# Softmax weights times values for two heads in one step, on the two halves of the array's columns

## The chip, the cores and the metric

One core of a Trainium2 chip runs the whole program. The metric is device time in microseconds (us), the median over executions. Five engines matter here: PE (TensorE, matmuls; its weight loads are shown apart as PEld), DVE (VectorE), ACT (ScalarE), POOL (GpSimd) and SP, which issues the weight loads.

## The reference, cut to what matters

Two transformer blocks over 256 tokens of width 1024. Three of their attentions have heads whose values are 64 wide, and these three are what the change touches:

```python
# first block, sliding window: 8 query heads over 2 key/value heads, d = 64
s = jnp.einsum('bnqhgd,bnkhd->bnhgqk', qb, kw).astype(jnp.float32) * scale
...
p = e / (jnp.sum(e, axis=-1, keepdims=True) + jnp.exp(sink - m))
o = jnp.einsum('bnhgqk,bnkhd->bnqhgd', p.astype(v.dtype), vw)

# second block, layer 0 (hybrid): 8 heads, values 64 wide
p = masked_softmax(s, kpos[None, :] <= qpos[:, None])
return jnp.einsum('bhqk,bkhd->bqhd', p.astype(v.dtype), v)

# second block, layer 1: 16 heads over 2 key/value heads, three branches added with gates
o_c = jnp.einsum('bgrqn,bngd->bqgrd', p_c.astype(dt), v_cmp)
o_s = jnp.einsum('bgrqk,bgqkd->bqgrd', p_s.astype(dt), vs)
o_w = jnp.einsum('bgrqk,bkgd->bqgrd', p_w.astype(dt), vw)
```

With 256 tokens the selected branch (`o_s`) and the window branch (`o_w`) of layer 1 are plain causal attentions; `o_c` is a small one over 15 compressed keys. Everything else is projections, feed-forwards, norms and residuals.

## The kernel before, in words

The weights (some 300 MB) are streamed from memory in units of 1 MB. Each unit is split into a high part (ACT, tile `whi`) and a low part (DVE, tile `wlo`, line 404), and a product with weights is three matmuls, high by high, low by high, high by low (tile `mm`). 24 such matmuls belong to one weight step. Attention works in plain float32, and a float32 matmul leaves two weight loads and two matmul records in the trace, one for each of its passes.

The program is a list of steps in one order, and each engine carries out its part of them in that order; nothing is rescheduled. For one head with 64 value columns there are four steps:

- S: `scores` (line 791) puts the mask and q·k into a PSUM tile `sc` (two buffers), and `softmax` (line 801) takes the maxima on DVE (`nm`, lines 806 and 807) and the exponentials on ACT (`p`);
- N: `scale_p` (line 834) inverts the sums on DVE (`r`, lines 829 and 831) and multiplies the weights by them (line 838);
- T: `transp` (line 841) turns the weights over with three matmuls against the identity (PSUM tile `pT`, two buffers) and copies them to `pTs` (three buffers), on DVE (line 330) or ACT in turn;
- P: `pv` (line 850) multiplies them with the values (tile `v` or `va`) into one half of the partitions of a PSUM tile `o`: 64 value columns are the stationary operand, so the product takes 64 of the array's 128 columns, the lower half for one head of a pair and the upper one for the other. All 256 queries take part with the first 128 keys, and the last 128 queries with the other keys. After the second head, `split_out` (line 885) takes `o` into two parts `oh` (ACT) and `ol` (DVE) for the output product.

`rounds` (line 271) makes the order: in round r it puts T of item r-3, P of item r-5, S of item r and N of item r-1 (lags 0, 1, 3, 5; for layer 1 of the second block the table `NLAGS` = 0, 1, 4, 6 is used, line 45). The three places are:

- the sliding window heads of the first block (`sP`, line 1142; list made at line 1154), 8 items, spread by `merge` among weight steps (line 1265);
- the hybrid layer (`mP`, line 1538; line 1548), 8 items, spread among four weight steps, then the last `HY` = 14 steps among two (line 1553);
- layer 1 (`nP`, line 1718; line 1740), 32 items in the order pair j, branch b, half g; six weight steps are put into rounds 0, 1, 4, 5, 10 and 13 (`NFILL`), and two more among the last `NS` = 20 steps (line 1749). After both branches of a pair of heads, one matmul with `cpT` and `vcz` adds the compressed branch to the same `o`.

Of the kernel before, what the change touches and what calls it, by code (L numbers as in the profile page):

```python
# [24 lines left out]
P = 128  # L25
# [25 lines left out]
# ------------------------------------------------------------------ host layout  # L51
def _tiles(w):
    """[K, M] -> [K/128, M/128, 128, 128]"""
    K, M = w.shape
    return w.reshape(K // P, P, M // P, P).transpose(0, 2, 1, 3)


def _units(seq):
    """sequence of [128, n] blocks (given as [T, 128, n]) -> [128, T * n], 16 tiles a unit"""
# [7 lines left out]
def pack_pairs(w):  # L67
    """column tiles in pairs, k outside the pair"""
    t = _tiles(w)
    K, M = t.shape[:2]  # L70
    t = t.reshape(K, M // 2, 2, P, P).transpose(1, 0, 2, 3, 4)
    return _units(t.reshape(-1, P, P))


def pack_cols(w):
    """column tiles one after the other, k inside"""
# [4 lines left out]
def early_order(K, M):  # L81
    """(column tile, row tile) in turn: the first half of the rows for the first half of the columns comes first"""
# [12 lines left out]
def pack_rows(w, kk):  # L95
    """kk row tiles a unit, all columns of each"""
# [5 lines left out]
def pack_ada(w):  # L102
    """for each modulation row, units of two row tiles"""
# [4 lines left out]
def cols(v):  # L108
    """[n * 128] -> [128, n]"""
# [131 lines left out]
# ------------------------------------------------------------------ kernel  # L241
# [6 lines left out]
class Two:  # L248
    """two [P, S] tiles seen as one [P, 2, S]"""
# [8 lines left out]
def merge(a, b):  # L258
    """two lists of steps, each in its order, spread evenly over one another"""
# [11 lines left out]
def rounds(n, *stages, lags=(0, 1, 3, 5)):  # L271
    """the stages of n items, each stage so many rounds behind the first; later stages first in a round"""
    out = []
    for r in range(n + lags[-1]):
        for k in (2, 3, 0, 1):
            i = r - lags[k]
            if 0 <= i < n:
                out += stages[k](i)
    return out


class Kernel:
# [12 lines left out]
    # ---- small helpers  # L295
# [6 lines left out]
    def t(self, name, shape=None, dt=F):  # L302
        """short-lived"""
# [16 lines left out]
    def table(self, func):  # L320
        """loads the table of a function ahead of its use"""
# [4 lines left out]
    def copy(self, out, in_):  # L326
        """PSUM -> SBUF on whichever of the two engines had less"""
# [19 lines left out]
    def mm3(self, out, w, x, start, stop, swap=False):  # L347
        """float32 product of operands in two parts; w stationary unless swap"""
# [7 lines left out]
    # ---- the stream of weights  # L356
    def stream_init(self, steps):
        """loads in the order of use, but raw units behind the next LEAD split ones"""
# [54 lines left out]
    def second(self):  # L413
        """the low part of the last split, one split behind its high part"""
# [35 lines left out]
    # ---- products with weights  # L450
    def pairs(self, name, x, kc, evac, unit0=0, npairs=None, st=None, head=0, tags=("mm", "mm"),
              biased=None):
        """steps: column tiles in pairs, k outside; evac(pair, psum [P, 2, S]); the first head pairs are of
        activations not yet normed (their norm's state in st), with the shift in two columns behind them"""
# [50 lines left out]
    def singles(self, name, x, kc, evac, early=False):  # L505
        """steps: column tiles one by one, k inside; evac(m, psum [P, S]); early: half of the columns start on
        the first half of the activations"""
# [25 lines left out]
    def rowsteps(self, name, x, width, evac, unit0=0, nk=8, kk=4, sub_k=2, tags=("mm", "mm")):  # L533
        """steps: the activations stationary, [tokens, width] out; evac(token block, psum)"""
# [18 lines left out]
    # ---- norms over the features (which lie on partitions)  # L553
    # The products that follow a norm start on x * gain; what the norm divides by is per token, so it is
    # applied to their results, or to the activations once it is there.
    def norm_part(self, st, c, n, xc, gain, dst=None):
        """one chunk's share of the sum of squares, and the chunk times its gain in two parts"""
# [67 lines left out]
    def along(self, out, by):  # L625
        """the factors of the tokens, which lie on partitions, along the free axis of every partition"""
# [3 lines left out]
    def norm_bc(self, st, scale=1.0):  # L630
        """what the norm multiplies by, along the tokens; and the results that waited for it"""
# [7 lines left out]
    def norm_apply(self, st, gain, shift, c0, c1):  # L639
        """the activations themselves, over those not normed"""  # L640
# [1186 lines left out]
```

## Time and profile before

| | |
|---|---|
| runs, median (lowest to highest) | 1501.49 us (1499.78 to 1502.46), 3 runs |
| profiled execution, span from first to last instruction | 1497.7 us |
| PE busy, weight loads busy | 97%, 92% |
| DVE, ACT, POOL busy | 71%, 61%, 42% |
| the sliding window heads' stretch of the trace, first P to behind the last | 75.30 to 114.70 us |
| the hybrid heads' stretch, first S to behind the last P | 699.70 to 735.60 us |
| layer 1's stretch, first P to behind the last | 1202.70 to 1278.20 us |

The profiled execution has no other time of its own than its span, which lies 3.8 us under the median of the runs. "Busy" of PE counts matmul records whose ends are modelled, so the time from one start to the next says more than the busy time.

### The profile page before, as it was taken

What the parts mean: (1) busy time and instruction counts of PE and PEld (TensorE: products, weight loads), DVE (VectorE), ACT (ScalarE), POOL (GpSimd) and SP (SyncE); (2) the same over time, 40 slices, a digit from 0 to 9 for tenths busy, and PEclk for the clock granted to TensorE, in tenths of its full rate; (3) what the DMA queues carried; (4) which work ended last, traced back from release to release, by engine and by line L of the source; (5) the groups of instructions that cost most, each with busy time, mean ns of one, the idle gap of its engine ahead of it and who ended that gap; (6) DMA issues with size and microseconds to landing.
All of it is one profiled execution on the core that took longest, in us unless ns stands there. A gap on an engine that the chain in (4) does not pass through costs nothing.

```text
span 1497.7 us, 28352 instructions
## 1 busy us (share of the span) xinstructions
PE 1454.4 (97%) x11478; PEld 1384.8 (92%) x11478; DVE 1056.4 (71%) x1643; ACT 918.8 (61%) x1666; POOL 635.8 (42%) x466
## 2 busy tenths in 40 slices
PE   8998999999999999998999999999999999999997
PEld 8887989999989989997899999899999877999997
DVE  7967767776658777679887676677665777764553
ACT  6546766777657567664677666576654555654442
POOL 3102433545874567753546659466553200500021
PEclk9999999999999999999999999999999999999999
DMA  8344646677665777654548777577754510355551
GB/s 316 117 141 165 211 159 226 245 268 277 250 253 194 292 255 272 253 195 165 182 172 289 275 277 259 204 274 279 288 215 175 197 57 5 137 197 183 184 174 51
DMA packets 46067, 312.00 MB, mean 208 GB/s; under 512 B 5232, under 2 KB 7024, under 8 KB 9072
## 3 DMA queue, kind: packets, MB, share of 16 engines
q1 hardware_dynamic: 45936, 310.19, 57.7%
q8 instruction: 90, 1.47, 0.4%
q14 instruction: 41, 0.34, 0.1%
HBM read 309.12 MB, written 1.05 MB: 207 GB/s over the span
## 4 chain that ended last, share of the span: by engine, by line
PE 69%; DVE 15%; ACT 7%; DMA 5%; issue 3%; POOL 2%; SPq 0%; POOLq 0%; ACTq 0%; DVEq 0%
PE mm L345 59%; DVE wlo L404 5%; DMA raw<-w 3%; PE o L345 3%; PE sc L345 2%; ACT whi L318 2%; POOL adacc L726 2%; ACT raw L318 1%; PE mmt L345 1%; DVE hlo L653 1%; PE pT L845 1%; DVE hlo L563 1%; PE ada L345 1%; DVE gl L342 1%; DMA raw<-w_up 1%
## 5 line engine op out<-in xcount | busy, mean ns | idle before, releaser
L404 DVE TENSOR_TENSOR wlo<-raw,whi 128x1024 fp32r<-128x1024 f32 (+2 forms) x438 | 625.5, 1434 | 51.0 <-ACT whi L318 50.4
L726 POOL TENSOR_TENSOR adacc<-adacc,raw 128x512 f32<-128x512 f32 x252 | 431.9, 1739 | 415.5 <-ACT raw L318 338.8
L345 PE MATMUL mm<-hlo,whi 128*128 128x256 f32 x1960 | 556.8, 284 | 4.5 <-DVE hlo L653 4.1
L345 PE MATMUL mm<-hhi,whi 128*128 128x256 f32 (+1 forms) x1960 | 558.4, 285 | 1.1 <-ACT whi L318 1.1
L345 PE MATMUL mm<-hhi,wlo 128*128 128x256 f32 (+1 forms) x1960 | 553.4, 282 | 4.6 <-DVE wlo L404 4.6
L318 ACT ACTIVATE whi<-raw 128x1024 fp32r<-128x1024 f32 (+2 forms) x438 | 453.1, 1044 | 112.6 <-DMA raw<-w 75.3
L345 PEld LDWEIGHTS mm<-hlo,whi 128*128 128x128 f32 x1960 | 370.1, 189 | 8.3 <-DVE hlo L653 5.6
L345 PEld LDWEIGHTS mm<-hhi,wlo 128*128 128x128 f32 x1960 | 371.2, 189 | 7.0 <-DVE wlo L404 6.6
L345 PEld LDWEIGHTS mm<-hhi,whi 128*128 128x128 f32 x1960 | 370.3, 189 | 5.1 <-issue 2.5
L345 PE MATMUL mm<-gh,whi 128*128 128x256 f32 x960 | 272.6, 284 | 0.0
L345 PE MATMUL mm<-gh,wlo 128*128 128x256 f32 x960 | 271.6, 283 | 0.0
L345 PE MATMUL mm<-gl,whi 128*128 128x256 f32 x960 | 271.6, 283 | 0.0
L345 PEld LDWEIGHTS mm<-gh,whi 128*128 128x128 f32 x960 | 184.2, 192 | 4.3 <-issue 3.4
L345 PEld LDWEIGHTS mm<-gl,whi 128*128 128x128 f32 x960 | 184.2, 192 | 0.0
L345 PEld LDWEIGHTS mm<-gh,wlo 128*128 128x128 f32 x960 | 184.2, 192 | 0.0
L318 ACT ACTIVATE raw<-raw,sc 128x512 f32<-128x512 f32 x252 | 166.9, 711 | 0.6 <-DMA raw<-ada 0.5
L1398 DVE TENSOR_TENSOR ft<-mm,ft 128x256 f32<-128x256 f32 x79 | 33.4, 423 | 111.6 <-ACT ft L318 111.4
L342 DVE TENSOR_TENSOR gl<-ft,gh 128x256 fp32r<-128x256 f32 x120 | 74.1, 628 | 46.0 <-ACT gh L318 45.8
L569 POOL TENSOR_SCALAR xg<-x,M 128x256 f32<-128x256 f32 x40 | 58.3, 1458 | 98.6 <-DVE x L1261 92.3
L318 ACT ACTIVATE p<-sc,nm 128x128 f32<-128x128 f32 (+1 forms) x120 | 49.9, 421 | 74.1 <-DVE r L829 29.4
L318 ACT ACTIVATE ft<-mm 128x256 f32<-128x256 f32 x79 | 29.8, 378 | 93.5 <-PE mm L345 93.5
L585 POOL TENSOR_TENSOR acc<-acc,sq 128x256 f32<-128x256 f32 x60 | 60.4, 1009 | 44.1 <-ACT sq L318 37.1
(298 smaller groups left out, 1908.4 us busy)
## 6 DMA issues: line engine op xcount, KB each, us to landing
raw<-w SPq DMA_DIRECT2D x132, 1024.0 KB, 4.9
raw<-ada SPq DMA_DIRECT2D x72, 1024.0 KB, 6.2
raw<-w_up SPq DMA_DIRECT2D x16, 1024.0 KB, 5.0
raw<-w_down SPq DMA_DIRECT2D x16, 1024.0 KB, 5.4
raw<-hy_in SPq DMA_DIRECT2D x8, 1024.0 KB, 4.9
raw<-w_in SPq DMA_DIRECT2D x6, 1024.0 KB, 8.0
raw<-nsa_in SPq DMA_DIRECT2D x6, 1024.0 KB, 4.9
raw<-w_ck SPq DMA_DIRECT2D x4, 1024.0 KB, 4.8
```

The lines of the kernel that those rows point to most:

```text
L318: return self.nc.scalar.activation(out, in_, func, **k)
L342: self.nc.vector.tensor_tensor(lo, src, hi.bitcast(F), OP.subtract)
L345: self.nc.tensor.matmul(out, lhsT, rhs, start=start, stop=stop, skip_group_check=True)
L404: self.behind = lambda hi=hi[:, :b - a], lo=lo[:, :b - a], src=src: self.nc.vector.tensor_tensor(lo, src, hi.bitcast(F), OP.subtract)
L563: self.deferred.append(lambda: nc.vector.scalar_tensor_tensor(lo, xc, gain(c), hi.bitcast(F), op0=OP.mult, op1=OP.subtract))
L569: nc.gpsimd.tensor_scalar(st["xg", c], xc, gain(c), None, op0=OP.mult)
L585: nc.gpsimd.tensor_tensor(acc, st["acc" + key], sq, OP.add)
L653: nc.vector.scalar_tensor_tensor(*last, op0=OP.add, op1=OP.subtract)
L726: nc.gpsimd.tensor_tensor(half, half, src, OP.add)
L845: self.nc.tensor.transpose(ps[:, s, :], src, self.eye)
L1398: nc.vector.tensor_mul(s, ps[:, 1, :], s)
```

## The change

`pv` takes two heads at once: the two matmuls over all queries for one head and the other, then the two over the last 128 queries. A new function `twos` makes the order: S and N stay one item each and at their rounds, T and P are made for two items at once, in the round in which the second of the two had them before, and P now stands ahead of T in a round. `sP`, `mP` and `nP` take two heads. The step lists get shorter by four, four and sixteen steps, and the counts `HY` and `NS` are left as they are. Comments and docstrings are removed too, and every line number behind them moves.

```diff
+def twos(n, *stages, lags):
+
+    out = []
+    for r in range(n + lags[-1]):
+        for k in (3, 2, 0, 1):
+            i = r - lags[k]
+            if 0 <= i < n and (k < 2 or i % 2):
+                out += stages[k](i) if k < 2 else stages[k](i - 1, i)
+    return out
...
-    def pv(self, o, v0, v1, pT, start=True, stop=True):
-        """o [64, 256] += (v.T @ p.T)"""
-        self.mm(o, v0, pT[:, :S], start=start, stop=False)
-        self.mm(o[:, P:], v1, pT[:, S:], start=False, stop=stop)
+    def pv(self, o, vs, pTs, start=True, stop=True):
+
+        half = [o[64 * n:64 * n + 64] for n in range(2)]
+        for n in range(2):
+            self.mm(half[n], vs[n][0], pTs[n][:, :S], start=start, stop=False)
+        for n in range(2):
+            self.mm(half[n][:, P:], vs[n][1], pTs[n][:, S:], start=False, stop=stop)
...
-        att = rounds(8, lambda n: [sS(hd[n])], lambda n: [sN(hd[n])], lambda n: [sT(hd[n])],
-                     lambda n: [sP(hd[n], *heads[n])])
+        att = twos(8, lambda n: [sS(hd[n])], lambda n: [sN(hd[n])], lambda n, m: [sT(hd[n]), sT(hd[m])],
+                   lambda n, m: [sP(heads[n][0])], lags=(0, 1, 3, 5))
...
-        at = rounds(8, lambda n: [mS(n)], lambda n: [mN(n)], lambda n: [mT(n)], lambda n: [mP(n)])
+        at = twos(8, lambda n: [mS(n)], lambda n: [mN(n)], lambda n, m: [mT(n), mT(m)], lambda n, m: [mP(n, m)],
+                  lags=(0, 1, 3, 5))
...
-        def nP(j, g, b):
-            def fn():
-                if g == 0 and b == 0:
+        def nP(j, b):
+            def fn():
+                if b == 0:
                     sw["o"] = self.otile()
-                v = lambda tb: vt[tb][:, b * P + 64 * g:b * P + 64 * g + 64]
-                self.pv(sw["o"][64 * g:64 * g + 64, :], v(0), v(1), sw.pop((j, g, b)), start=b == 0, stop=False)
-                if g == 1 and b == 1:
+                v = lambda g, tb: vt[tb][:, b * P + 64 * g:b * P + 64 * g + 64]
+                self.pv(sw["o"], [(v(g, 0), v(g, 1)) for g in range(2)], [sw.pop((j, g, b)) for g in range(2)],
+                        start=b == 0, stop=False)
+                if b == 1:
                     self.mm(sw["o"], cmp["v"][j % 4 // 2][:, j % 2, :], cmp["pT", j // 4], start=False)
-                if g == 1 and b == 1:
                     o[j] = self.split_out(sw["o"], "o")
             return Step(fn)
...
-        att = rounds(32, first, lambda n: [nN(*items[n])], lambda n: [nT(*items[n])], lambda n: [nP(*items[n])],
-                     lags=NLAGS)
+        att = twos(32, first, lambda n: [nN(*items[n])], lambda n, m: [nT(*items[n]), nT(*items[m])],
+                   lambda n, m: [nP(items[n][0], items[n][2])], lags=NLAGS)
```

The order of the rows on SP and POOL does not change. In the rows below `identb` and `maskvz` are the mask's part of S, `pT` is T, `o<-pTs` is P; `x2` means two in a row.

**PE, in the middle of layer 1.** Before, one round stands so:

```order
L345 LDWEIGHTS identb
L345 MATMUL sc<-maskvz,identb 128x2x128
L345 MATMUL sc<-kz,q 128x128
L345 MATMUL sc<-kz,q 128x256
L845 MATMUL pT<-cst,p_15002 128x128
L845 MATMUL pT<-cst,p_15003 128x128 x2
L345 MATMUL o<-pTs,v 64x256
L345 MATMUL o<-pTs,v 64x128
L345 MATMUL o<-cpT,vcz 128x256
```

The change has two scores in a row, then P of a pair, then T of a pair:

```order
L356 LDWEIGHTS identb
L356 MATMUL sc<-maskvz,identb 128x2x128
L356 MATMUL sc<-kz,q 128x128
L356 MATMUL sc<-kz,q 128x256
L356 MATMUL o<-pTs,v 64x256 x2
L356 MATMUL o<-pTs,v 64x128 x2
L356 MATMUL o<-cpT,vcz 128x256
L856 MATMUL pT<-cst,p_14964 128x128
L856 MATMUL pT<-cst,p_14965 128x128 x2
L856 MATMUL pT<-cst,p_15002 128x128
L856 MATMUL pT<-cst,p_15003 128x128 x2
```

The four matmuls of two heads stand together, once in two rounds where one head's two stood in every round, and the transposes stand behind them.

**PE, at the end of layer 1.** Before, the last three heads follow one another behind the last transposes:

```order
L845 MATMUL pT<-cst,p_15569 128x128
L845 MATMUL pT<-cst,p_15570 128x128 x2
L345 MATMUL o<-pTs,v 64x256
L345 MATMUL o<-pTs,v 64x128
L345 MATMUL o<-pTs,v 64x256
L345 MATMUL o<-pTs,v 64x128
L345 MATMUL o<-pTs,v 64x256
L345 MATMUL o<-pTs,v 64x128
L345 MATMUL o<-cpT,vcz 128x256
```

With the change, P of the last pair stands right behind that pair's own transposes:

```order
L356 MATMUL o<-pTs,v 64x256 x2
L356 MATMUL o<-pTs,v 64x128 x2
L856 MATMUL pT<-cst,p_15535 128x128
L856 MATMUL pT<-cst,p_15536 128x128 x2
L856 MATMUL pT<-cst,p_15569 128x128
L856 MATMUL pT<-cst,p_15570 128x128 x2
L356 MATMUL o<-pTs,v 64x256 x2
L356 MATMUL o<-pTs,v 64x128 x2
L356 MATMUL o<-cpT,vcz 128x256
```

The pair at the top of these rows stands right behind its own transposes too, which are not shown.

**PE, at the end of the hybrid heads.** Before:

```order
L845 MATMUL pT<-cst,p 128x128 x3
L345 MATMUL o<-pTs,v 64x256
L345 MATMUL o<-pTs,v 64x128
L345 MATMUL o<-pTs,v 64x256
L345 MATMUL o<-pTs,v 64x128
L345 MATMUL o<-pTs,v 64x256
L345 MATMUL o<-pTs,v 64x128
L345 MATMUL mm<-oh,whi 128x256
```

And with the change:

```order
L856 MATMUL pT<-cst,p 128x128 x3
L356 MATMUL o<-pTs,v 64x256 x2
L356 MATMUL o<-pTs,v 64x128 x2
L856 MATMUL pT<-cst,p 128x128 x6
L356 MATMUL o<-pTs,v 64x256 x2
L356 MATMUL o<-pTs,v 64x128 x2
L356 MATMUL mm<-oh,whi 128x256
```

Here too the last two pairs stand right behind transposes whose result they read.

## Rows read from the trace of the kernel before

**Rows 1.** The page's first part: the span, then busy time, share and instructions of PE.

```profile
span 1497.7 us, 28352 instructions
PE 1454.4 (97%) x11478; PEld 1384.8 (92%) x11478; DVE 1056.4 (71%) x1643; ACT 918.8 (61%) x1666; POOL 635.8 (42%) x466
```

**Rows 2.** The chain that ended last: shares by engine, then by line.

```profile
PE 69%; DVE 15%; ACT 7%; DMA 5%; issue 3%; POOL 2%; SPq 0%; POOLq 0%; ACTq 0%; DVEq 0%
PE mm L345 59%; DVE wlo L404 5%; DMA raw<-w 3%; PE o L345 3%; PE sc L345 2%; ACT whi L318 2%; POOL adacc L726 2%; ACT raw L318 1%; PE mmt L345 1%; DVE hlo L653 1%; PE pT L845 1%; DVE hlo L563 1%; PE ada L345 1%; DVE gl L342 1%; DMA raw<-w_up 1%
```

**Rows 3.** Tile `o` alone: matmul records of P, durations in ns, first and last start.

```profile
L345 PE MATMUL o<-pTs,v x160: 272/326/431, 715.4 to 1277.7; 128*64 128x256 f32 x80, 128*64 128x128 f32 x80
L345 PE MATMUL o<-pTs,va x32: 272/326/430, 75.4 to 114.5; 128*64 128x256 f32 x16, 128*64 128x128 f32 x16
```

**Rows 4.** Timeline of PE, layer 1, two rounds: start, time, operation.

```profile
1255.37 0.49 PE L845 MATMUL pT<-cst,p 128*128 128x128 f32 x3
1255.79 0.86 PE L345 MATMUL o<-pTs,v 128*64 128x256 f32 x4
1256.59 0.28 PE L345 MATMUL sc<-maskvz,identb 128*128 128x256 bf16 x1
...
1257.36 0.49 PE L845 MATMUL pT<-cst,p 128*128 128x128 f32 x3
1257.79 0.86 PE L345 MATMUL o<-pTs,v 128*64 128x256 f32 x4
```

**Rows 5.** Timeline of PE, layer 1, before the first P: transposes, then scores.

```profile
1194.21 0.49 PE L845 MATMUL pT<-cst,p 128*128 128x128 f32 x3
1194.54 0.27 PE L345 MATMUL sc<-maskvz,identb 128*128 128x256 bf16 x1
```

**Rows 6.** Timeline of PE, sliding window heads: two heads between weight matmuls.

```profile
109.70 0.28 PE L345 MATMUL mm<-hml,whi 128*128 128x256 f32 x1
109.82 0.28 PE L345 MATMUL mm<-hmh,wlo 128*128 128x256 f32 x1
110.03 0.88 PE L345 MATMUL o<-pTs,va 128*64 128x256 f32 x8
110.84 0.39 PE L345 MATMUL mm<-hmh,whi 128*128 128x256 f32 x1
```

**Rows 7.** Timeline of the last three heads of layer 1; the last row from 1276.3 to 1276.4.

```profile
1275.87 0.55 PE L845 MATMUL pT<-cst,p 128*128 128x128 f32 x3
1276.35 1.58 PE L345 MATMUL o<-pTs,v 128*64 128x256 f32 x12
1276.46 0.56 DVE L330 COPY pTs<-pT 128x384 f32<-128x384 f32 x1 [0.76 <-PE pT L845]
1277.87 0.70 PE L345 MATMUL o<-cpT,vcz 128*128 128x256 f32 x2
...
1276.35 0.44 PE L345 MATMUL o<-pTs,v 128*64 128x256 f32 x2
```

**Rows 8.** Timeline of PE, the last three heads of the hybrid layer, and what follows.

```profile
734.05 1.58 PE L345 MATMUL o<-pTs,v 128*64 128x256 f32 x12
...
735.56 0.39 PE L345 MATMUL mm<-oh,whi 128*128 128x256 f32 x1
```

**Rows 9.** Windows: stretch, length, busy PE, PEld, DVE, ACT, POOL, clock, DMA share, GB/s.

```profile
1225.04:1261.69 36.65, 36.21 (x221) 25.67 (x219) 27.47 (x108) 19.92 (x78) 1.54 (x3) 1.00 0.09 29
1253.80:1257.79 3.99, 3.99 (x26) 2.79 (x25) 3.27 (x15) 2.21 (x9) 0.00 (x0) 1.00 0.00 2
75.30:114.70 39.40, 39.40 (x280) 34.64 (x279) 25.52 (x54) 15.86 (x32) 0.00 (x0) 1.00 0.41 138
699.70:735.60 35.90, 33.68 (x243) 28.47 (x241) 31.89 (x70) 22.95 (x60) 14.15 (x10) 1.00 0.45 157
```

**Rows 10.** Waits of PE in the hybrid stretch: us in total, times, longest.

```profile
PE pT L845 <- DVE p L838: 1.2, 2, 0.8
PE mm L345 <- ACT yh L318: 0.9, 1, 0.9
```

More of the change, by code (lines that the diff above doesn't have):

```diff
@@ L1140, in sT, with sP @@
             return Step(fn)
-        def sP(hd, j, kv):
+        def sP(j):
             def fn():
-                if kv == 0:
-                    sw["o"] = self.otile()
-                v = lambda tb: va[0][:, tb * P + 64 * kv:tb * P + 64 * kv + 64]
-                self.pv(sw["o"][64 * kv:64 * kv + 64, :], v(0), v(1), sw.pop(hd))
-                if kv == 1:
-                    o[j] = self.split_out(sw["o"], "o")
+                ot = self.otile()
+                v = lambda kv, tb: va[0][:, tb * P + 64 * kv:tb * P + 64 * kv + 64]
+                self.pv(ot, [(v(kv, 0), v(kv, 1)) for kv in range(2)], [sw.pop(j + 4 * kv) for kv in range(2)])
+                o[j] = self.split_out(ot, "o")
             return Step(fn)
@@ L1536, in mT, with mP @@
             return Step(fn)
-        def mP(hd):
+        def mP(*hds):
             def fn():
-                e = hd % 2
-                if e == 0:
-                    sw["o"] = self.otile()
-                vv = lambda tb: v[tb][hd // 4][:, (hd % 4) * 64:(hd % 4) * 64 + 64]
-                self.pv(sw["o"][64 * e:64 * e + 64, :], vv(0), vv(1), sw.pop(hd))
-                if e == 1:
-                    y[4 + hd // 2] = self.split_out(sw["o"], "o")
+                ot = self.otile()
+                vv = lambda hd, tb: v[tb][hd // 4][:, (hd % 4) * 64:(hd % 4) * 64 + 64]
+                self.pv(ot, [(vv(hd, 0), vv(hd, 1)) for hd in hds], [sw.pop(hd) for hd in hds])
+                y[4 + hds[0] // 2] = self.split_out(ot, "o")
             return Step(fn)
-        at = rounds(8, lambda n: [mS(n)], lambda n: [mN(n)], lambda n: [mT(n)], lambda n: [mP(n)])
+        at = twos(8, lambda n: [mS(n)], lambda n: [mN(n)], lambda n, m: [mT(n), mT(m)], lambda n, m: [mP(n, m)],
+                  lags=(0, 1, 3, 5))
         ysrc = (lambda k: y[k][0], lambda k: y[k][1])
```

## Prediction

> **What bounds the kernel now.** I read the page's first part, then the chain, then PE's timeline in the three places, and the windows of those places last. PE is busy 97% of a span of 1497.7 us [rows 1], and 69% of the chain that ended last is PE, 3% of it on line 345 with tile `o` [rows 2]. So what leaves PE's queue leaves the time, wherever no other engine is close behind. P has 160 + 32 matmul records [rows 3], four for each of 48 heads. In the sliding window stretch PE is busy for all 39.40 us and DVE for 25.52; in the hybrid stretch PE for 33.68 of 35.90 and DVE for 31.89; in a long stretch of layer 1 without weight steps, 36.65 us, PE for 36.21 and DVE for 27.47 [rows 9]. The first and the third are PE's; in the second DVE is nearly as full, and PE waits there already [rows 10].
>
> **What one head costs on PE today.** In a round of layer 1 P starts at 1255.79 and the next scores at 1256.59: 0.80 us [rows 4]. The transposes ahead of it take 0.42 us (1255.37 to 1255.79), while transposes followed by scores take 0.33 (1194.21 to 1194.54) [rows 5]. So 0.09 us of the switch into the half-width product lies ahead of P, and a head costs 0.89 us.
>
> **What a pair will cost.** The old order has this case already, by accident, where P of two heads meets without work between. Two sliding window heads run from 110.03 to 110.84, eight records in 0.81 us, and the weight matmul ahead of them takes 0.21 us where its neighbour takes 0.12 [rows 6]: 0.90 us for two heads, as much as one head costs alone. The same shows in the last three heads of layer 1: twelve records from 1276.35 to 1277.87, 1.52 us, where three heads apart would take 2.40 [rows 7]. Two of those records have started before 1276.40, 0.05 us after the first [rows 7], when no pass of 256 columns can have ended (about 0.21 us each, worked out under C): the two halves of the columns do run at the same time. The hybrid heads end in a run of three too, 734.05 to 735.56, 1.51 us [rows 8].
>
> The Trainium skill speaks against the size of this: "TensorE: Matmul & The Clock Gate", Part 3 (packing small matmuls), says that matmuls start and end strictly in program order. By that rule the second pass of the first head would hold up the first pass of the second, and the sum would be that of rival C; the trace does not agree here (eight records in 0.81 us, two started within 0.05 us), and the measured 0.90 us is used.
>
> **The sum on PE.** By the timeline 40 heads stand alone, one pair and two threes stand together. Before: 40 x 0.89 + 0.90 + 2 x (0.09 + 1.52) = 39.7 us. After: 24 pairs x 0.90 = 21.6 us. Saved: 18.1 us, of which 13.0 in layer 1 (29 x 0.89 + 1.61 - 16 x 0.90), 2.6 in the sliding window heads (6 x 0.89 + 0.90 - 4 x 0.90) and 2.5 in the hybrid ones (5 x 0.89 + 1.61 - 4 x 0.90). Scores, transposes and weight matmuls stay the same in number and kind. So do the instructions of DVE, ACT, POOL and SP; the loads follow the freeing of buffers, and the DMA engines are 5 to 45% busy in these stretches [rows 9], or less, so they follow along.
>
> **What is new: transposes with their product right behind.** In four places P now follows its own T: two at the end of layer 1, two at the end of the hybrid heads. The copy of `pT` to SBUF is then on the path. Today's last copy ends at 1276.46 + 0.56 = 1277.02, 1.15 us behind the start of its transposes at 1275.87 [rows 7], and two other heads' products cover it. P could start 0.42 us behind them, so each place waits 0.73 us: 4 x 0.73 = 2.9 us, 1.5 of it in layer 1. Bounds: nothing, if other work gets between, and 1.2 us a place if the copy also stands behind one DVE operation of its own length.
>
> **What is new: DVE close behind.** A double round of layer 1 took 3.99 us (1253.80 to 1257.79) with 3.27 us of DVE work [rows 9]. PE will need 3.99 - 0.88 = 3.11 (two single heads, 1.78, become one pair, 0.90). DVE is then 0.16 us short. Double rounds that end a pair of heads carry another product on PE and leave DVE that time, so half of 16 are short: 8 x 0.16 = 1.3 us. Over the stretch of 36.65 us with 16 heads PE needs 36.65 - 8 x 0.88 = 29.6 us and DVE 27.47 [rows 9]; so the bound below is nothing, and the one above is in the rivals.
>
> **Place by place.** Sliding window: 2.6 us, DVE has room. Layer 1: 13.0 - 1.5 - 1.3 = 10.2 us. Hybrid: 2.5 - 1.5 = 1.0 us; but DVE is 89% busy there, and PE already waits for it and for ACT by 1.2 and 0.9 us [rows 10], so I take half, 0.5 us. It may be -1, if those waits grow by as much as they are, and 2.5, if neither they nor the new ones show. Sum: 13.3 us. The profiled span would fall from 1497.7 to 1484.4 us; it lies 3.8 us under the median of the runs, 1501.5, which would fall to **1488.2 us**.
>
> **Rivals.**
>
> A. *The forecast*: pairs at 0.90 us, few waits, 1484 to 1492 us. Chance 0.65.
>
> B. *DVE takes over layer 1.* With the transposes in bursts, DVE gets maxima of two score tiles, products with `r` and copies at once, and a double round goes at DVE's pace with a hop between engines in it, say 3.6 us instead of 3.11 (halfway between what DVE needs, 3.27, and today's 3.99). The saving is then 0.39 us a double round: 16 x 0.39 - 1.5 = 4.7, with 2.6 and 0.5 elsewhere 7.8 us: 1493.7 us. For it: 3.27 of 3.11. Against it: DVE is free of such pressure in rounds with weight steps, and in the long stretch it would be 93% busy (27.47 of 29.6), not over. Chance 0.17. The Trainium skill's "TensorEngine Tiling (Array Packing)", section PSUM Bottleneck, warns of just this: tiling speeds up TensorE and not the emptying of PSUM.
>
> C. *Only partial overlap.* If the order by heads matters and passes of the two halves queue behind each other, one pass of 256 columns more stands in a pair. A single head's 0.80 us holds two passes of 256, two of 128 columns and some 0.16 of switching, so such a pass is 0.64 / 3 = 0.21 us: 24 x 0.21 = 5.0 us less saved, 1493.2 us. Against it: rows 6 and 7. Chance 0.08.
>
> D. *Slower: P waits for a late copy everywhere.* Between T and P of a pair lie only two groups of scores, each 0.77 us (1256.59 to 1257.36) [rows 4], and no longer a round with other products. The copy needs 1.15 us and P comes 0.42 + 1.54 = 1.96 us behind the transposes, so there is 0.81 us of slack. If DVE is more than that behind when the copy's turn comes, all 14 pairs of layer 1 that are not priced above wait, and above 0.81 + 13.3 / 14 = 1.8 us of backlog the whole gain is gone. At 2.0 us, little over half a double round of DVE work, each waits 1.2: 14 x 1.2 = 16.8 us, 1505.0 us. Against it: in DVE's order the copy stands ahead of the maxima of its own round, and with two score buffers PE cannot run far ahead of DVE. Chance 0.05.
>
> E. *The change does not do what it says*: the halves run one behind the other and only the switching is halved. A pair is then 2 x 0.64 + 0.25 = 1.53 us where two heads are 1.78: 24 x 0.25 = 6.0, less 2.9 of waits and 1.3 of DVE, 1.8 us: 1499.7 us, no change. Rows 6 and 7 speak against it. Chance 0.05.
>
> **How the numbers follow.** The predicted time is A's, 1488.2 us. A's upper bound of gain, 18.1 us without any new wait, is 1483.4; its lower bound, with all waits at their upper bounds (4 x 0.47 = 1.9 more) and the hybrid at -1, is 1491.6. B and C lie at 1493 to 1494. The range 1484.0 to 1495.0 holds A, B and C but for their edges and leaves out D and E, 0.10, and some 0.08 of the edges. 0.2%, 3.0 us, is about what a measurement of this kernel can tell from no change. A, B and C are faster by more (0.90), E is the same (0.05), D slower (0.05).
>
> **What would show it.** Right: P's records in pairs, eight in 0.81 us or thereabouts, 24 groups and none of four; PE's time from T to T in a double round of layer 1 at 3.1 to 3.6 us where it was 3.99; a wait of PE for the copies of `pTs` in four places, some 0.7 us each; the layer 1 stretch shorter by about 10 us, the sliding window one by 2.6, the hybrid one by less than 2. Wrong: groups of eight that take 1.1 us or more (C, E); PE idle behind DVE's `nm` or ACT's `p` in every double round (B); PE idle ahead of most `o` groups (D). The forecast fails if the layer 1 stretch loses less than 6 us, or if a later stretch gives back what the earlier ones gained.

## The result, and the profile after

The changed kernel takes 1492.66 us (median of 6 runs, 1489.76 to 1496.87) where the kernel before takes 1500.65 beside it: a ratio of 0.9946, 95% interval 0.9928 to 0.9965. Timed a second time it took 1492.50 us (7 runs) against 1498.02, ratio 0.9966 [0.9953, 0.9979]. It is faster, and the time lies in the range; but 8.0 us (5.5 the second time) are gained where 13.3 were forecast.

The profiled span fell from 1497.7 to 1489.9 us. The page's first part, as in [rows 1]: engine, busy time, share, instructions.

```profile
span 1489.9 us, 28338 instructions
...
PE 1437.3 (96%) x11478; PEld 1374.9 (92%) x11478; DVE 1059.5 (71%) x1643; ACT 918.9 (62%) x1666; POOL 633.6 (43%) x466
```

PE has as many instructions as before and 17.1 us less work (1454.4 in [rows 1]), near the 18.1 that were forecast for it. The span lost 7.8 us: some 9 us of PE's saving came back as PE's idle time.

To see where, take the start of one and the same weight matmul in both traces and subtract. The table does this at the ends of the three places, for all profiled runs (us, run minus before; the last column is the mean granted clock from 722 to 726 us, behind a wait in the hybrid stage). In every row with less than 1.00 the clock fell to 0.50; the fall began at another moment each time.

| run | sliding window | hybrid | layer 1 | clock |
|---|---|---|---|---|
| forecast | -2.6 | -0.5 | -10.2 | |
| the change | -1.27 | +2.57 | -8.28 | 1.00 |
| the change again | -1.29 | +3.92 | -8.31 | 0.50 |
| hybrid undone | -1.26 | -0.04 | -8.31 | |
| one half | -1.27 | +3.93 | -4.75 | 0.76 |
| by heads | -1.25 | +3.93 | -8.20 | 0.51 |
| covers | -1.25 | +2.93 | -8.07 | 0.79 |
| first hybrid pairs twice | -1.27 | +3.03 | -8.31 | 0.67 |
| T single | -1.75 | +2.56 | -8.77 | 1.00 |
| copies on ACT | -1.25 | +3.34 | -9.28 | 0.64 |
| T single, hybrid undone, last cover | -1.77 | 0.00 | -8.91 | |
| the same, copies on ACT | -1.77 | -0.86 | -10.81 | |

Where the same code runs the same difference comes back within some 0.1 us, but for the hybrid stage. That stage goes with the clock, and it varies besides: 3.34 and 3.93 us with the clock down, and 0.00 and -0.86 us in the last two rows, whose hybrid layer is the same. So, outside that stage, these differences tell more than the totals, which vary by several us. (Between the hybrid stage and 858 us every run gains 1.75 us at a wait for a load, also the one with the hybrid layer undone; that was not followed up.)

**The pairs cost what was forecast.** Tile `o` alone, as in [rows 3]:

```profile
L356 PE MATMUL o<-pTs,v x160: 272/351/431, 717.0 to 1269.4; 128*64 128x256 f32 x80, 128*64 128x128 f32 x80
L356 PE MATMUL o<-pTs,va x32: 272/326/430, 78.8 to 112.8; 128*64 128x256 f32 x16, 128*64 128x128 f32 x16
```

PE's timeline, one double round of layer 1 (start, time, operation; compare [rows 4]):

```profile
1222.74 0.87 PE L356 MATMUL o<-pTs,v 128*64 128x256 f32 x8
1223.55 0.88 PE L856 MATMUL pT<-cst,p 128*128 128x128 f32 x6
1224.26 0.27 PE L356 MATMUL sc<-maskvz,identb 128*128 128x256 bf16 x1
1224.37 0.82 PE L356 MATMUL sc<-kz,q 128*128 128x128 f32 x4
1225.02 0.27 PE L356 MATMUL sc<-maskvz,identb 128*128 128x256 bf16 x1
1225.13 0.82 PE L356 MATMUL sc<-kz,q 128*128 128x128 f32 x4
1225.88 0.87 PE L356 MATMUL o<-pTs,v 128*64 128x256 f32 x8
```

Eight records take 0.80 us from start to the next start (1222.74 to 1223.55), and 19 of the 24 groups do so; the other five wait for something. The double round takes 3.14 us (1222.74 to 1225.88), and two others take 3.14 and 3.18. The forecast had 3.11. In these three DVE keeps up. In two more it does not: they take 3.41 and 3.78 us, and DVE is busy for 95% and 96% of them (stretch, length, busy PE, PEld, DVE, ACT, POOL, clock, DMA share, GB/s):

```profile
1203.20:1206.61 3.41, 3.30 (x25) 2.34 (x24) 3.25 (x15) 2.44 (x8) 0.00 (x0) 1.00 0.75 257
1247.99:1251.77 3.78, 3.32 (x25) 2.33 (x24) 3.62 (x16) 2.21 (x9) 0.00 (x0) 1.00 0.01 2
```

**What PE waits for now.** The waits of PE in the three places, hybrid, sliding window and layer 1 in this order: us in total, times, longest.

```profile
PE mm L356 <- ACT yh L329: 2.7, 1, 2.7
PE pT L856 <- DVE p L849: 1.8, 2, 0.9
PE o L356 <- DVE pTs L341: 0.5, 1, 0.5
PE sc L356 <- ACT p L329: 0.4, 1, 0.4
...
PE mm L356 <- DVE vd L347: 0.8, 1, 0.8
...
PE cT L1704 <- ACT pTs L329: 1.6, 1, 1.6
PE sc L356 <- ACT p L329: 1.3, 2, 0.9
PE o L356 <- ACT pTs L329: 0.6, 2, 0.3
```

Few and long, and not in every round. In [rows 10] the first of these, `yh`, was 0.9 us. Where they come from shows in the windows of the kernel before (columns as in the last rows): the sliding window heads' first part, and the stretch of layer 1 with the second group of the compressed branch.

```profile
62.00:82.00 20.00, 20.00 (x113) 16.87 (x112) 18.51 (x47) 10.68 (x26) 0.00 (x0) 1.00 0.31 106
1234.00:1243.80 9.80, 9.80 (x64) 7.27 (x64) 8.35 (x34) 4.45 (x18) 1.54 (x3) 1.00 0.00 0
```

The matching stretch of layer 1 and the hybrid stage after the change:

```profile
1230.58:1240.33 9.75, 7.32 (x52) 5.21 (x52) 8.76 (x34) 4.19 (x16) 1.54 (x3) 1.00 0.00 0
698.30:737.10 38.80, 33.21 (x242) 27.51 (x240) 35.39 (x70) 22.96 (x60) 13.70 (x10) 1.00 0.46 167
```

In the kernel before, DVE was 93% busy in the first stretch (62 to 82 us) and 85% in the second (1234 to 1243.8 us), beside a PE that never stopped. Both are far above the means of the whole stretches in [rows 9] (65% and 75%), from which the forecast read that DVE had room. The waits of the changed kernel stand there. But a full DVE is not enough to make one: from 97 to 102 us and from 1220 to 1225 us the kernel before has DVE at 92% too (4.62 of 5.00 us), and no wait of PE came up there with the change.

The hybrid row says something else besides: DVE has 70 instructions, as in [rows 9], and is busy for 35.39 us with them instead of 31.89. They have become longer, by 3.5 us together; the account of the hybrid stage below comes back to this.

### The profile page after: what moved, and what is told of

It is laid out like the page before. It is cut to its first block, busy times and chain, and to the rows that moved or that the text cites. A ratio compares the mean times of both kernels' runs of the same rounds, so it can differ in the third digit from the quotient of the medians.

```text
span 1489.9 us, 28338 instructions
## 1 busy us (share of the span) xinstructions
PE 1437.3 (96%) x11478; PEld 1374.9 (92%) x11478; DVE 1059.5 (71%) x1643; ACT 918.9 (62%) x1666; POOL 633.6 (43%) x466
## 3 DMA queue, kind: packets, MB, share of 16 engines
q8 instruction: 90, 1.47, 0.4%
## 4 chain that ended last, share of the span: by engine, by line
PE 64%; DVE 16%; ACT 8%; DMA 7%; issue 2%; POOL 1%; SPq 0%; POOLq 0%; ACTq 0%; DVEq 0%
PE mm L356 57%; DVE wlo L415 6%; DMA raw<-w 4%; ACT whi L329 2%; ACT raw L329 2%; PE sc L356 2%; PE o L356 1%; DVE p L849 1%; POOL adacc L737 1%; PE mmt L356 1%; DVE hlo L664 1%; DMA raw<-w_up 1%; DMA raw<-w_down 1%; DVE gl L353 1%; ACT p L329 1%
```

## Experiments

Every kernel starts from the changed one, and its diff is against that. Five of them were timed once only (one half 1498.48 us, by heads 1493.52, first hybrid pairs twice 1494.38, T single 1494.18, copies on ACT 1494.24), so they are read by their stages and not by these totals.

### One half for both heads: do the halves run at the same time?

```diff
-        half = [o[64 * n:64 * n + 64] for n in range(2)]
+        half = [o[n:n + 64] for n in at]
...
-                        start=b == 0, stop=False)
+                        start=b == 0, stop=False, at=(0, 0) if b else (0, 64))
```

> In layer 1 the pairs of the window branch (8 of 16) put both heads' products into the lower half of the columns, so that the second head's product of these pairs is added into the first head's rows and missing from its own. Same number of matmuls, same order, same switches into and out of half-width products; only the two halves can no longer run side by side. Theory (the halves run at the same time): each of the 8 groups of eight records takes 0.80 + 0.64 = about 1.44 us instead of 0.80 (two passes of 256 and two of 128 columns more, 0.64 us as worked out for one head), and layer 1 becomes 8 x 0.64 = 5.1 us longer, less where PE waited for DVE anyway (4 to 5). Rival (the halves never overlap, and the pair is cheap because it switches once): the groups stay at 0.80 us, the stage within 0.5 us.

PE's timeline of such a pair:

```profile
1220.48 1.51 PE L356 MATMUL o<-pTs,v 128*64 128x256 f32 x8
1221.92 0.70 PE L356 MATMUL o<-cpT,vcz 128*128 128x256 f32 x2
```

1.44 us from start to the next start, in each of the eight groups whose products share a half, and 0.80 in those of the other branch (1.22 in one that waits). So the halves run at the same time, and that is worth 0.64 us a pair. Layer 1 became 3.5 us longer (-4.75 where it was -8.28), not 5.1, and less than the 4 to 5 that the expectation allowed for waits: the other 1.6 us came out of PE's waits. Already here PE's time is not the only bound of this layer.

### By heads: does the order in a pair matter?

```diff
-        for n in range(2):
-            self.mm(half[n], vs[n][0], pTs[n][:, :S], start=start, stop=False)
         for n in range(2):
+            self.mm(half[n], vs[n][0], pTs[n][:, :S], start=start, stop=False)
             self.mm(half[n][:, P:], vs[n][1], pTs[n][:, S:], start=False, stop=stop)
```

> Everywhere the four matmuls of a pair are put out by head (256 and 128 queries of one head, then 256 and 128 of the other) instead of in turn. Theory: the two halves keep their own queues of passes, so the order between them is nothing; groups of eight records take 0.80 to 0.82 us as with the change, and the whole span stays within 1 us. Rival (strict program order): the second head's first pass stands behind all of the first head's passes, so half of the overlap is lost; a pair then takes 1.0 to 1.4 us, 24 x 0.2 to 0.6 = 5 to 14 us more.

PE's timeline of a pair, then PE's records of `o` from 1215.29 to 1215.70 us by shape (busy us, mean ns, idle before):

```profile
1215.29 0.88 PE L356 MATMUL o<-pTs,v 128*64 128x256 f32 x8
1216.10 0.88 PE L856 MATMUL pT<-cst,p 128*128 128x128 f32 x6
...
L356 PE MATMUL o<-pTs,v 128*64 128x256 f32 x4 | 0.7, 405 | 0.0
```

The pair takes 0.81 us (1215.29 to 1216.10) with the second head's first matmul third of four in the queue. Sliding window and layer 1 are as long as with the change, within 0.1 us, and the hybrid stage as long as when the change was run again. The whole span is 1.8 us longer than the changed kernel's first, where 1 was allowed: 1.4 of it is the hybrid stage with its lowered clock. The order "in turn" is not needed, and rival C is out. The last row shows why: all four passes over 256 columns, two of either head, have started before any pass over 128, though the first head's matmul over 128 stands ahead of the second head's first in the queue. By the Trainium skill's rule of strict program order ("TensorE: Matmul & The Clock Gate", Part 3) the passes of the second head would have queued behind the first; these rows do not agree.

### The hybrid layer undone

```diff
-        at = twos(8, lambda n: [mS(n)], lambda n: [mN(n)], lambda n, m: [mT(n), mT(m)], lambda n, m: [mP(n, m)],
-                  lags=(0, 1, 3, 5))
+        at = rounds(8, lambda n: [mS(n)], lambda n: [mN(n)], lambda n: [mT(n)], lambda n: [mP(n)])
```

`mP` takes one head again, and `pv1` is the old `pv`.

> Only the hybrid layer gets its old order back (one head at a time, P of a head apart from the other's); the sliding window heads and layer 1 stay changed. Theory: the changed order costs the hybrid stage 2.5 us net (the trace of the changed kernel stands 1.0 us ahead of the one before at the stage's start and 1.5 us behind it at its end), because transposes and products of a pair come in bursts and meet DVE late. Then this stage is as long as before, 2.5 us shorter than with the change; a weight load further on (843 to 865 us) may take back up to 1.8 of that, so the whole time falls by 0.7 to 2.5 us. Rival 1: the loss is an accident of this profiled execution (a late DMA); then the stage is as long as with the change, within 0.5 us, and the time the same. Rival 2: pairing saves its 2.5 us here too and something moved in from an earlier stage costs 5; then the stage becomes longer without pairs, by up to 2.5 us.

The stage is as long as before (-0.04), and the kernel takes 1489.39 us (5 runs; ratio 0.9935 [0.9914, 0.9956]). Both rivals are out: pairing costs this stage 2.6 us, in a place where PE's own work was forecast to fall by 2.5. The waits are those of the kernel before again, `yh` 0.9 and `p` 1.2 us, and so is DVE's busy time, 31.86 us in the stage's 35.90 (columns as above):

```profile
697.98:733.88 35.90, 33.75 (x243) 28.54 (x241) 31.86 (x69) 22.92 (x59) 13.97 (x10) 1.00 0.44 155
```

Its total lies 10.0 us under its runs of before, where the change lay 8.0 and 5.5 under its own: the totals agree with the stage and are too rough to size it.

### The change again, and the clock behind a wait

> The changed kernel itself, once more. Its first profile showed a granted clock of 1.00 behind PE's 2.98 us wait for yh, and four other kernels with the same hybrid order and a wait as long showed 0.50 to 0.80 there and a stage that was 1.3 us longer. Theory (the fall is a matter of the execution, not of those kernels' edits): this profile may show either, and the hybrid stage costs 2.5 us over the kernel before with the clock up or about 3.9 with it down, nothing in between without a partial fall; layer 1 gains 8.3 us again. Rival (the edits did it): clock 1.00 and 2.5 us again.

Nothing is edited here. The waits are the same, and in the hybrid stage so is the gap ahead of the product with `yh` (2.97 us where the first trace has 2.98). Windows of this run, from the start of that gap:

```profile
719.00:722.00 3.00, 0.69 (x2) 0.52 (x3) 2.41 (x7) 1.16 (x3) 0.00 (x0) 0.79 0.77 287
722.00:726.50 4.50, 4.50 (x21) 4.44 (x22) 4.46 (x7) 2.88 (x8) 2.52 (x2) 0.50 0.31 93
726.50:728.00 1.50, 1.50 (x7) 0.96 (x6) 0.81 (x4) 0.00 (x0) 0.00 (x0) 0.65 0.99 410
728.00:732.00 4.00, 4.00 (x36) 3.53 (x35) 3.26 (x9) 3.69 (x12) 0.00 (x0) 1.00 0.13 53
```

PE had hardly any matmul in the 3 us ahead, and the granted clock fell to 0.50, the lower of its two levels (1.2 GHz). The stage cost 3.92 us instead of 2.57: 1.35 us more, in which the other differences between the two executions are netted. In the first trace the same gap left the clock at 1.00. Of the eight runs with a gap of 2.4 us or more there, two kept the clock and six lost it for a while. So the same edits gave either: the fall hangs on the execution, and it is a second price of the wait. In the kernel before, and with the hybrid layer undone, the gap is 1.2 us and the clock stays.

### The first hybrid pairs twice: who sets the product with `yh`?

```diff
-                self.pv(ot, [(vv(hd, 0), vv(hd, 1)) for hd in hds], [sw.pop(hd) for hd in hds])
+                vs, ts, twice = [(vv(hd, 0), vv(hd, 1)) for hd in hds], [sw.pop(hd) for hd in hds], hds[0] < 4
+                self.pv(ot, vs, ts, stop=not twice)
+                if twice:
+                    self.pv(ot, vs, ts, start=False)
```

> In the changed kernel's hybrid layer the products of the first two pairs are put out twice, adding 16 records, some 1.6 us of PE, ahead of the product that waits for yh (the values of those four heads come out doubled). Theory: the start of that product is set by the chain on DVE and ACT that ends in yh, so what PE saves ahead of it is not seen: PE's wait there falls from 2.98 to about 1.4 us and the stage stays as long as with the change, within 0.5 us, or becomes 1.3 us shorter than in the runs where the granted clock fell to 0.5 behind that wait, if the shorter wait keeps the clock up. Rival (PE's own work sets this stage): the wait stays at 2.9 us and the stage becomes 1.6 us longer.

The expectation put both pairs ahead of that product; in the trace only the first pair stands there. Its 16 records take 1.45 us instead of 0.80, so 0.65 us were added, and PE's gap ahead of the product fell from 2.98 to 2.36: by 0.62. So what PE saves or spends ahead of `yh` doesn't show. The stage is 0.46 us longer than the one with the clock up and 0.9 shorter than the one with the clock down; the clock fell too, but for a shorter time (0.67 from 722 to 726 us, 0.80 from 726 to 728, 1.00 behind).

What sets `yh` is DVE, as the rows have it. Its timeline in the changed kernel, with POOL's and the wait on PE:

```profile
715.77 1.41 DVE L849 TENSOR_SCALAR p<-p,r 128x256 f32<-128x256 f32 x1
717.11 2.30 DVE L415 TENSOR_TENSOR wlo<-raw,whi 128x1024 fp32r<-128x1024 f32 x1
719.33 0.41 DVE L1451 TENSOR_TENSOR cvv<-mm,cu 128x256 f32<-128x256 f32 x1
...
715.76 2.56 POOL L737 TENSOR_TENSOR adacc<-adacc,raw 128x512 f32<-128x512 f32 x2 [8.08 <-issue]
732.52 2.49 POOL L737 TENSOR_TENSOR adacc<-adacc,raw 128x512 f32<-128x512 f32 x2 [7.17 <-issue]
...
722.12 0.38 PE L356 MATMUL mm<-yh,whi 128*128 128x256 f32 x1 [2.70 <-ACT yh L329]
```

From `cvv` (719.33) to `yh` (ACT, 721.65) the chain takes 2.3 us, and it begins when DVE has done `p` and `wlo`. Those take 1.41 and 2.30 us here, elsewhere in this layer 0.35 and 1.22, and POOL's two additions stand beside them (715.76 to 718.32). In the kernel before one such instruction of this chain is longer (`ca`, 1.46 us instead of 0.35, at 720.47, beside POOL's addition), here two are: by these rows, about 1.0 us of the 1.8 us by which the gap grew.

### Covers: other work between T and P

```diff
-NCMP = (2, 3, 5), (1, 3, 5)
+NCMP = (2, 3, 5), (1, 3, 6)
...
-        steps += merge(at[:-HY], zr[2:]) + merge(at[-HY:], outs[:2]) + outs[2:]
+        steps += merge(at[:-HY], zr[2:]) + at[-HY:-4] + outs[:1] + at[-4:-1] + outs[1:2] + at[-1:] + outs[2:]
...
-        steps += att[:-NS] + merge(att[-NS:], outs[:2]) + outs[2:]
+        steps += att[:-4] + outs[:1] + att[-4:-1] + outs[1:2] + att[-1:] + outs[2:]
```

> Three moves in the changed kernel's list of steps: in the hybrid layer and at the end of layer 1 the two output weight steps, which were spread over the last 14 and 20 steps, are put between T and P of the last two pairs, where P followed its own transposes; and in layer 1 the transposes of the second compressed group (cT) move from the second-last scores of a round with pairs to a round that has no burst of transposes. Theory: P waits 0.8 to 0.9 us in each of four places for its copies, and cT waits 1.6 us for a transpose buffer that the pair's two T have taken. Then layer 1 becomes 1.6 + 2 x 0.85 = 3.3 us shorter, the hybrid stage 1.5 us shorter, and the time falls by 3 to 5 us. Rival (DVE's or ACT's backlog is what is waited for, whatever stands in between): the waits move to the next step that needs the same engine; each stage gains less than 0.5 us, and the time stays.

A miss in the sum (1493.74 us, ratio 0.9960 [0.9946, 0.9974]), with one part right. The last two pairs of layer 1 now take 0.80 us where they took 1.22 and 1.20, and they no longer wait for the first copy behind their transposes: 1.8 us in all. But layer 1 gained nothing (-8.07). The moved `cT` waits no longer, while the scores ahead of it and the transposes behind it do (1.20 and 2.14 us from start to start, where 1.94 stood with the change), and a P waits 0.66 us in a round that the weight steps have left:

```profile
1242.94 0.27 PE L356 MATMUL sc<-maskvz,identb 128*128 128x256 bf16 x1 [0.82 <-ACT p L329]
...
1243.70 0.39 PE L1704 MATMUL cT<-cst,cs 128*128 128x128 f32 x2
...
1247.35 0.55 PE L856 MATMUL pT<-cst,p 128*128 128x128 f32 x3 [1.87 <-ACT cpT L329]
```

The wait moved, as the rival said. In the hybrid stage the covers took 1.0 us off (2.93 against 3.92, both with a lowered clock) where 1.5 were expected; runs with no edit there differ by 0.6 themselves.

### Single transposes

```diff
-            if 0 <= i < n and (k < 2 or i % 2):
+            if 0 <= i < n and k == 2:
+                out += stages[k](i, i)[:1]
+            elif 0 <= i < n and (k < 2 or i % 2):
                 out += stages[k](i) if k < 2 else stages[k](i - 1, i)
```

> In all three places the products stay in pairs, but each head's transposes stand in a round of their own again (order in a round: P, T, S, N), so that a round has one set of transposes and not two or none. Theory: layer 1's missing 2 us and the sliding window's missing 1.3 us are lost to the bursts of two sets of transposes, which take both transpose buffers at once (cT waited 1.9 us where it waited 0.7 before; the transposes at 82.45 us waited 1.1 us) and leave P right behind its own transposes. Then the pairs still take 0.80 us, the wait of cT falls to 0.7 us or less, only one place in layer 1 is left where P waits for its copies (0.9 us less), layer 1 gains 10 to 11 us over the kernel before where it gained 8.3, and the sliding window stretch 2 to 2.6 where it gained 1.3. The hybrid stage loses 1.2 us less, for one late copy less. Rival (DVE's and ACT's total work is what is missing, whatever the order): the same waits come back at other rows; layer 1 gains 8 to 8.6 us, the sliding window 1.3.

Mostly a miss. The sliding window gained 1.75 us instead of 1.27, layer 1 8.77 instead of 8.28, the hybrid stage nothing. The wait at `cT` stands as it was, only one row further on (a gap of 1.92 us behind `cT`, and one of 1.28 behind an earlier set of transposes), and the releaser is now DVE:

```profile
1241.30 0.38 PE L1706 MATMUL cT<-cst,cs 128*128 128x128 f32 x2
1243.33 0.55 PE L858 MATMUL pT<-cst,p 128*128 128x128 f32 x3 [1.65 <-DVE pTs L343]
```

Nor did the last two pairs of layer 1 gain: they take 1.61 and 1.51 us, where 1.22 and 1.20 stood. So the bursts of transposes cost some 0.5 us net in each of two places, and the waits that are left stand at whatever row comes, as the rival has it. Whether DVE's work is what they wait for is what the next run asks.

### All copies of layer 1 on ACT

```diff
-                sw[j, g, b] = self.transp(sw[j, g, b], None if g or b else self.act)
+                sw[j, g, b] = self.transp(sw[j, g, b], self.act)
```

> In the changed kernel's layer 1 all copies of pT to pTs go to ACT (20 of 32 do so now, 12 go to DVE), and nothing else changes. That takes 12 x 0.47 us = 5.6 us from DVE and gives ACT about as much. Theory: what layer 1 lost in its middle (1.25, 1.94, 0.84 and 0.49 us of PE's gaps, 2.9 us more than before) is DVE's backlog, which piles up behind the compressed branch's 2.5 us of extra DVE work; then these gaps shrink by 1 to 2.5 us together, and the layer gains 9.3 to 10.8 us over the kernel before where it gained 8.3. Rival 1 (the hops from engine to engine are what is waited for, not DVE's load): the gaps stay within 0.4 us together. Rival 2 (ACT becomes the bound: p, oh and all copies there take some 2.6 to 3.0 of 3.1 us in a double round): PE waits for p or pTs of ACT in most double rounds and the layer gains less than 8.

Layer 1 gained 9.28 us instead of 8.28, at the low end of what was expected, and neither rival came: of the four gaps 0.49 us is gone, 0.84 is 0.38, 1.94 is 1.47, and 1.25 stays at 1.27. Its waits:

```profile
PE cT L1704 <- ACT pTs L329: 1.1, 1, 1.1
PE sc L356 <- ACT p L329: 0.9, 1, 0.9
PE o L356 <- ACT pTs L329: 0.6, 2, 0.3
```

DVE's load in this layer is thus part of the price. The Trainium skill's "TensorEngine Tiling (Array Packing)", PSUM Bottleneck, warns that the emptying of PSUM may become the bound and advises both engines for it; this run agrees with the warning, by 1.0 us, while its share between the engines is another. What is left of the two long gaps stands with the compressed branch, whose own DVE work (the rows of `cs` and `cmx`) wasn't moved.

### Versions that beat both

The first has the hybrid layer undone, single transposes in the other two places, and the second output weight step between the last T and the last P of layer 1:

```diff
-        steps += att[:-NS] + merge(att[-NS:], outs[:2]) + outs[2:]
+        steps += att[:-NS] + merge(att[-NS:-1], outs[:1]) + outs[1:2] + att[-1:] + outs[2:]
```

> A candidate that should beat both: the hybrid layer in its old order, the sliding window and layer 1 with products in pairs and single transposes, and in layer 1 the second output weight step between the last transposes and the last product. Theory: 2.5 us from the hybrid layer (as its own run showed), 1.3 from the sliding window, 2 to 3 from layer 1, so 5 to 7 us under the changed kernel: about 1486 us, a ratio of 0.990 to 0.992 to the kernel before. Rival (waits only move): 1489 to 1490 us, as with the hybrid layer undone alone.

1487.48 us (6 runs), ratio 0.9924 [0.9912, 0.9936]: between theory and rival. Layer 1 gained 8.91 us, hardly more than with single transposes alone.

The second adds the copies on ACT:

> The hybrid layer in its old order, products in pairs with single transposes in the other two places, the second output weight step between the last transposes and the last product of layer 1, and all copies of pTs in layer 1 on ACT. Theory (DVE's backlog in the middle of layer 1): 1 to 2.5 us under the same kernel with copies on both engines, 1485 to 1486.5 us, ratio 0.990 to 0.992. Rival (ACT becomes the bound): 1488 us or more.

1485.82 us (5 runs, 1483.15 to 1487.13), ratio 0.9912 [0.9898, 0.9927]; the span is 1482.8. Layer 1 gained 10.81 us, 1.9 more than without the edit; the hybrid stage gained 0.86 with no edit of its own. PE's waits in layer 1:

```profile
PE pT L858 <- ACT pTs L331: 1.1, 1, 1.1
PE sc L358 <- ACT p L331: 0.7, 1, 0.7
PE pT L858 <- ACT cpT L331: 0.3, 1, 0.3
```

This is the fastest kernel of the study.

## Why the prediction was right and wrong

The mechanism on PE was right, and three of the terms that come off its saving were too small. 1492.66 us lies in the range, but not in the forecast's own band of 1484 to 1492, and above 1491.6, its sum with every new wait at its upper bound: the range holds the result because it was drawn to hold rivals B and C as well. As far as the forecast's own sum goes, that is luck.

**Right: what a pair costs.** "0.90 us for two heads" held: 0.80 us and the 0.09 ahead of it, in 19 of 24 groups, and one half for both heads gave 0.64 us back, the very passes that the working of C counted. Of PE's saving of 18.1 us, 17.1 show in its busy time. C and E are out by the two runs on pairs, D by the few waits ahead of `o`.

**Right in kind, near in size: P behind its own T.** "Each place waits 0.73 us." In the hybrid layer it is 0.71 us a place (1.51 us for a group, 0.80 without), since the second head's first pass waits for its copy:

```profile
735.59 1.37 PE L356 MATMUL o<-pTs,v 128*64 128x256 f32 x6
735.70 0.56 DVE L341 COPY pTs<-pT 128x384 f32<-128x384 f32 x1 [0.20 <-PE pT L856]
```

735.70 + 0.56 = 736.26 us is when the second half can start. In layer 1 it is 0.9 us a place, as P waits for the first head's copy (ACT, 0.3 us each in the waits above) and then for the second's (1.22 and 1.20 us for a group): 1.8 us where 1.5 were taken.

**Wrong in layer 1: "half of 16 are short: 8 x 0.16 = 1.3 us".** Three double rounds are not short at all (3.14 and 3.18 us). Four gaps of 0.49, 1.25, 1.94 and 0.84 us stand in their place. 0.22 us is the usual distance between scores, so they hold 3.6 us, and the like before held 0.8: 2.9 us net. 13.0 - 1.8 - 2.9 = 8.3, and 8.28 was measured. The two longest lie with the compressed branch, where DVE has some 2.5 us of work that the double round of [rows 9] doesn't have; the other two lie in the double rounds of 3.41 and 3.78 us. So the term of 1.3 us measured 2.9: one double round of DVE's work, 3.27 us, was taken for all of them. B named the engine rightly and the shape wrongly: its 1493.7 us is nearer to the result than 1488.2, but its double round of 3.6 us came twice only (3.41 and 3.78).

**Wrong in the sliding window: "2.6 us, DVE has room".** 1.27 us were gained. Behind one set of transposes the weight matmul starts 1.11 us late (the wait for `vd` above), and behind two `rot` the scores start 0.24 us late each; 2.6 - 1.0 - 0.5 is 1.1. No run took DVE's work away here, so that it is DVE's load that is waited for is read from the rows. DVE's 25.52 of 39.40 us in [rows 9] is true and hides 18.51 of 20.00 us just ahead of that stretch and at its start.

**Wrong in the hybrid stage: "I take half, 0.5 us. It may be -1".** It is -2.57, and -3.92 when the clock falls. The stage's own working named the right waits and took too little for them. By the rows: `yh` takes 1.8 us more (a gap of 2.98 instead of 1.17), the two late copies 1.4, a set of transposes behind `p` 1.1 at 735.22 (DVE's two `p` took 2.42 us there, beside POOL's additions at 732.52, and 0.55 where POOL is idle), the pair at 726.32 1.2 (1.97 us instead of 0.80), and a wait of 0.6 before is gone: 4.9 us, against 2.5 saved on PE and 2.6 lost in the end.

```profile
732.74 2.42 DVE L849 TENSOR_SCALAR p<-p,r 128x128 f32<-128x128 f32 x2
735.22 0.44 PE L856 MATMUL pT<-cst,p 128*128 128x128 f32 x2 [0.90 <-DVE p L849]
```

The forecast counted the new waits at DVE's old durations. DVE's work itself became longer: 35.39 us for 70 instructions instead of 31.89, and 31.86 again with the pairs undone. In the new order all six additions of POOL from 715 us on stand beside a `p` or a `wlo`, which are 0.8 to 1.1 us longer each; of the six in the kernel before, two stand beside a longer instruction of DVE. That pairing causes the loss is shown by undoing it, and that PE's time ahead of `yh` is hidden by doubling a pair; how the sum divides, and that POOL is the reason for DVE's longer instructions, is read from the rows. The forecast's own mark, "if a later stretch gives back what the earlier ones gained", came true: this stage gave back twice what the sliding window had won.

Together the three places gave 7.0 us instead of 13.3, and the rest of the span 0.8. The median fell by 8.0.

## What to carry to other kernels

Before you take work off the engine that is full, read the other engines' busy share in slices as short as the waits you fear, a few rounds each, and not over the stretch. A slice where a second engine is nearly full is a place where the saving may come back as idle time: here it did in slices at 93% and 85%, and did not in two others at 92%. In the hybrid stage, at 89% [rows 9], it came back with interest, and there the second engine's own instructions had become longer in the new order. And of instructions that you pull together into a group, look up the latest operand: the group waits for that one, as the last pairs did for their second copy.

## What was not expected of the hardware

- **Two halves of the columns run at the same time for float32 in two passes, in both orders of the queue that were tried**: 0.80 us in turn, 0.81 by heads, 1.44 when both are in one half. A second pair right behind the first adds only 0.65 us (16 records in 1.45).
- **A gap of 3 us on PE can cost more than itself**: behind the same gap the granted clock was 1.00 once and 0.50 for several us another time, 1.35 us of difference, net, in the same kernel.
- **DVE beside POOL**: `p` over 256 columns took 1.41 us instead of 0.35, `wlo` 2.30 instead of 1.22, with POOL's `adacc` additions at the same time. Each is 1.1 us longer, about one addition of 1.28 us. The same code shows it come and go: of the last two versions, whose hybrid layer is the same, one has two `p` of 2.72 us together at 702.61 and a gap of 0.73 us ahead of the transposes that need them, the other has 1.59 us at 703.71 and no such gap; its stage is 0.86 us shorter. The Trainium skill's "SBUF — State Buffer", Who interferes with whom, has a lock on ports that the two engines share, under which the later of two such instructions waits for the earlier; these rows agree, but no run took the additions away.
